# dt from the full normed x while x is prepared, in place of its hi and lo parts in a unit of its own

## Chip, cores and metric

The kernel runs on one core of a Trainium2 chip. The metric is the device time of one execution in microseconds (us). Three runs of the kernel before took 1902.75, 1903.54 and 1903.64 us; the median is 1903.54 us.

## The reference, cut to what matters

One layer of a hybrid decoder is computed for a prompt of 256 positions and for 8 sample positions that share all weights (264 columns in all). One projection of the normed input feeds every branch; 32 of its 13,856 columns are dt:

```python
def _in_proj(x, norm_mix, w_in, ...):
    h = _rmsnorm(x, norm_mix)
    q, k, v, z, xbc, dt, qm, g = jnp.split(h @ w_in, _split_points(IN_SPLITS), axis=-1)
    ...
def _ssd(xbc_raw, z, dt_raw, ...):
    dt = jax.nn.softplus(dt_raw.astype(f32) + dt_bias.astype(f32))...
    acs = jnp.cumsum(dt * a, axis=2)
    ...
```

dt sets the decays of the scan (SSD), so `_ssd` needs it before the first chunk. Keys and values of 256 memory tokens (`_mem_kv`) come from another normed input and another weight, `w_mem_kv`, and depend on nothing of x.

## The kernel before, in words

**Tiling.** Activations lie with features on the 128 partitions: 16 feature tiles (`KT`) of 128 x 264. A weight is loaded in units of 128 x 1024 (two feature tiles by 512 columns), and each unit is split into `hi` (rounded to the fast matmul type, ScalarE, L181) and `lo` (the rest, VectorE, L182). A product of two fp32 operands is three fast products: hi by hi, lo by hi, hi by lo (`group`, L303). The activations are split alike: the normed x is kept as `hh` (hi) and `hl` (lo).

**Units.** The list `units` holds the whole program's weight units in the order in which TensorE takes them: 32 units for memory keys and values (`mem_group`, products `pmem`, 128 x 512), then the projection (products `pin`, 128 x 264), then the up-projections, the output and the feed-forward. The main loop (L1746) keeps up to four units' loads (`feed`, L268, issued on SyncE) and three units' splits ahead of TensorE. PSUM has five banks for such products (`dps`) and three for side work (`sps`).

**Side work.** Everything else (norms, attention, the scan) are generators in two queues (`side`, `slow`, L1719 to L1735). After each unit the loop takes a step of them; some groups wait for a task (`XDRAIN`, L1432). A scheduler with its own model of time then orders the instructions of each engine; what is marked `keep_in_program_order` keeps its own order among such marks, yet other instructions may be set between.

**x.** `prep_x` (L465) runs beside the memory units. It sums squares, finds the reciprocal norm (`rsqrt`, VectorE), spreads it over the partitions (product `rbx`, L492, copied to `rb` by ScalarE, L494), and then for each of the 16 feature tiles transposes x on TensorE (`xT`, L505, two transposes each), copies it from PSUM (`xr`, ScalarE, L506), multiplies it with the norm (`xn`, VectorE, L508, a `t1` buffer of one tile) and splits it into `hh` and `hl` (L509). The loop demands its end at unit 30 (L1754); the first `pin` unit is unit 32.

**dt.** `dt_group` (L1446) is one unit of its own, between the group of C and the first group of x columns. It loads the 128 x 512 weight of dt's 32 columns (16 feature tiles), copies it as it is (L284, "whole") and makes 32 products in full fp32, each with 32 output rows: for each of four rounds, four feature tiles with `hh`, then the same four with `hl`. The four products of a round write four different quarters of the 128 output partitions of `pdt`, so `task_dt` (L1188) later sums the quarters (`dtT`, L1200). ScalarE copies `pdt` to `dtraw` (L1465). `task_dt` runs after the tasks of B and C.

**Quarter-width products.** A product with 32 output rows is built for a quarter of TensorE's columns (128 x 32); the quarter is the one of its output partitions. `ssq` (L676) is of the same kind.

Of the kernel before, what the change touches and what calls it, by code (L numbers as in the profile page):

```python
# [8 lines left out]
F32 = mybir.dt.float32  # L9
# [3 lines left out]
AF = mybir.ActivationFunctionType  # L13
# [5 lines left out]
P = 128  # L19
# [3 lines left out]
NT = NP + NS  # L23
KT = D // P
# [53 lines left out]
def tile_hybrid_decoder_step(  # L78
# [33 lines left out]
    def ev(name):  # L112
        return tp.tile([P, 4, NT], F32, tag="ev", name=nm(name), bufs=4)

    def const(shape, name, dt=F32, tag=None):
        return cp.tile(shape, dt, tag=tag or name, name=name)
# [29 lines left out]
    def t1(name, dt=F32):  # L146
        return tp.tile([P, NT], dt, tag="t1", name=nm(name), bufs=4)
# [5 lines left out]
    def dps(name):  # L153
        return pd.tile([P, 512], F32, tag="d", name=nm(name))
# [122 lines left out]
    def do_split(n):  # L277
        if n < state["split"]:
            return
        raw = raws.pop(n)  # L280
        hi = wp.tile([P, 1024], F32R, tag="hi", name=nm("hi"), bufs=3)
        lo = wp.tile([P, 1024], F32R, tag="lo", name=nm("lo"), bufs=3)
        if units[n].get("whole"):
            act(hi.bitcast(F32)[:, 0:512], raw[:, 0:512], AF.Copy)  # L284
        elif units[n].get("perm"):
            for k in range(2):
                v = [t[:, k * 512:(k + 1) * 512].rearrange("p (r a d) -> p a r d", r=4, a=2) for t in (hi, lo)]
                s = raw[:, k * 512:(k + 1) * 512].rearrange("p (a r d) -> p a r d", a=2, r=4)
                state["split_at"], state["rest_at"] = split(v[0], v[1], s)
        else:  # L290
            for k in range(2 if n == 0 else 1):
                c = slice(512 * k, 512 * k + 512) if n == 0 else slice(0, 1024)
                with tc.issue_after(state["memh", k if n == 0 else 1].ins):
                    state["split_at"], state["rest_at"] = split(hi[:, c], lo[:, c], raw[:, c])
        parts[n] = (hi, lo)
        state["split"] = n + 1
# [165 lines left out]
    for n, (t, h) in ((9, (1, 0)), (10, (0, 1)), (11, (1, 1))):  # L462
        behind[n] = [lambda t=t, h=h: load_x_rows(t, h)]

    def prep_x():  # L465
        xs = x_t["s"]
        jk = t2("jkx", BF16)
        ss = tiny("ssx", 6)
        act(jk[:, 0:P], xs, AF.Square, accum_out=ss[:, 4:5])
        for t in range(2):  # L470
            for h in range(2):
                act(jk, x_t[t, h], AF.Square, accum_out=ss[:, 2 * t + h:2 * t + h + 1])
            yield 0.5
        sel = tiny("sel", NS)
        V.tensor_reduce(sel, ident.rearrange("p (k b) -> p b k", b=NS), axis=AX.X, op=ALU.add)
        V.tensor_scalar(sel, sel, ss[:, 4:5], None, op0=ALU.mult)
        ps = sps("xn")
        tr(ps[:, 0:P], xs)
        mm(ps[:, P:P + NS], ones, sel)
        v = tiny("vx", 10)  # L480
        V.tensor_tensor(v[:, 0:2], ss[:, 0:4:2], ss[:, 1:4:2], op=ALU.add)
        V.tensor_copy(v[:, 2:10], ps[:, P:P + NS])
        xsT = t1("xsT")[:, 0:P]
        act(xsT, ps[:, 0:P], AF.Copy)
        V.tensor_scalar(v, v, 1.0 / D, EPS, op0=ALU.mult, op1=ALU.add)
        r = rsqrt(v, 10)
        yield 1.5
        dg = t1("dgx")[:, 0:256]
        for t in range(2):
            V.tensor_scalar(dg[:, t * P:(t + 1) * P], ident, r[:, t:t + 1], None, op0=ALU.mult)  # L490
        ps = sps("rbx")
        mm(ps[:, 0:NP], ones, dg)  # L492
        rb = t1("rb")
        act(rb[:, 0:NP], ps[:, 0:NP], AF.Copy)  # L494
        V.tensor_copy(rb[:, NP:NT], r[:, 2:10])
        yield 0.5
        for q in range(4):
            raw = ev("xr")
            V.tensor_copy(raw[:, :, NP:NT], xsT[:, 32 * q:32 * q + 32].rearrange("p (c b) -> p c b", b=NS))
            for c in range(4):  # L500
                k = 4 * q + c
                h, o = k // 8, (k % 8) * P
                ps = sps("xT")
                for t in range(2):
                    tr(ps[:, t * P:(t + 1) * P], x_t[t, h][:, o:o + P])  # L505
                act(raw[:, c, 0:NP], ps[:, 0:NP], AF.Copy)  # L506
                tm = t1("xn")
                V.scalar_tensor_tensor(tm, raw[:, c], g_mix[:, k:k + 1], rb, op0=ALU.mult, op1=ALU.mult)  # L508
                split(hh(k), hl(k), tm)  # L509
                yield 0.6  # L510
            nc.gpsimd.dma_start(xT_d[:, 4 * q:4 * q + 4], raw)


    tri = const([P, P], "tri")
# [580 lines left out]

    ssd = {}
    dt_tok = const([P, 64], "dt_tok")
    last = const([P, 11, 24], "last")
    acs_tok = const([P, 64], "acs_tok")
    wf = const([P, 96], "wf")  # L1100

# [6 lines left out]
    def conv(ct, raw, dst):  # L1108

        acc = t4("acc").rearrange("p (c n) -> p c n", c=4)  # L1110
        for c in range(4):
            ch = ct + c
            act(acc[:, c], raw[:, c], AF.Identity, scale=cw[:, 72 + ch:73 + ch], bias=c_bias[:, ch:ch + 1])
            for k in (2, 1, 0):
                o = 3 - k
                V.scalar_tensor_tensor(acc[:, c, o:NP], raw[:, c, 0:NP - o], cw[:, k * 24 + ch:k * 24 + ch + 1],
                                       acc[:, c, o:NP], op0=ALU.mult, op1=ALU.add)
            yield 1.3
        V.tensor_tensor(acc[:, :, NP:NT], acc[:, :, NP:NT], pre[:, ct:ct + 4], op=ALU.add)
        act(dst, acc, AF.Silu)  # L1120
        V.tensor_copy(last[:, :, ct:ct + 4].rearrange("p r c -> p c r"), raw[:, :, NP - 3:NT])
        if ct == 12:
            ps = sps("rawT")
            lf = last.rearrange("p r c -> p (r c)")
            for i, (o, n) in enumerate(((0, 72), (72, 96), (168, 96))):
                tr(ps[0:n, i * P:(i + 1) * P], lf[:, o:o + n])
            rows = t2("rawT")
            act(rows[0:72, 0:P], ps[0:72, 0:P], AF.Copy)
            act(rows[0:96, P:3 * P], ps[0:96, P:3 * P], AF.Copy)
            nc.scalar.dma_start(p_conv[0, 0].rearrange("r (c n) -> (r c) n", n=P), rows[0:72, 0:P])  # L1130
            for i in range(2):
                nc.scalar.dma_start(s_conv[0, 4 * i:4 * i + 4, 2].rearrange("b (c n) -> b c n", n=P),
                                    rows[0:96, (i + 1) * P:(i + 2) * P])
        yield 0.3
# [8 lines left out]
        return f  # L1143

    def task_b():
        ssd["B"] = const([P, 4, NT], "BT")
        yield from conv(16, ssd["Braw"], ssd["B"])
        bt = const([P, 2, 512], "Btok")
        for t in range(2):
            ps = sps("Btok")  # L1150
            for g in range(4):
                tr(ps[:, g * P:(g + 1) * P], ssd["B"][:, g, t * P:(t + 1) * P])
            act(bt[:, t], ps, AF.Copy)
        ssd["Btok"] = bt
        yield 0.2
# [32 lines left out]
    def task_dt():  # L1188
        ssd["dsc"] = const([P, 16, 17], "dsc", tag="nd")
        s3 = const([P, 3, 16, NS], "s3", tag="kT")  # L1190
        ssd["xsS"], ssd["zsS"], ssd["ysS"] = (s3[:, i] for i in range(3))
        raw = ssd["dtraw"]
        x = tiny("dtx", 64)

        sm = t1("dtsum")[:, 0:P]
# [233 lines left out]
            split(ssd[f"s{g}"][:, 0:4, NP:NT], ssd[f"s{g}"][:, 4:8, NP:NT], t[:, 4 * g:4 * g + 4])  # L1429
        yield 3  # L1430

    XDRAIN = ("W", "dt", "N0", "N1")  # L1432

    def x_group(g):
        h_group(C_X + 512 * g, after_xbc(f"x{g}"), before=lambda: side.drain(XDRAIN[g]))
# [1 line left out]
    def z_group(g, before=None, middle=None):  # L1437
# [4 lines left out]
            ssd[f"z{g}"] = z  # L1442
            side.ready.add(f"z{g}")
        h_group(C_Z + 512 * g, f, before=before, middle=middle)

    def dt_group():  # L1446
        def loads(raw):
            return [(raw[:, 0:512].rearrange("p (k n) -> p k n", k=KT),
                     w_in[0, :, C_DT:C_DT + 32].rearrange("(k p) n -> p k n", p=P))]

        def prod(hi, lo):

            ps = dps("pdt")[:, 0:NT]
            w = hi.bitcast(F32)
            for j in range(4):
                for x in (hh, hl):
                    for q in range(4):
                        k = 4 * j + q
                        tc.keep_in_program_order(mm(ps[32 * q:32 * q + 32], w[:, 32 * k:32 * k + 32], x(k).bitcast(F32),
                                                    start=j == 0 and x is hh, stop=j == 3 and x is hl))  # L1460
            ssd["dtps"] = ps

        def after():
            raw = t1("dtraw")
            act(raw, ssd["dtps"], AF.Copy)  # L1465
            ssd["dtraw"] = raw
            side.ready.add("dt")

        units.append(dict(loads=loads, prod=prod, after=after, whole=True))


    mg = {}

# [80 lines left out]
        gates_ssd(i)  # L1554
    h_group(C_B, after_xbc("B"))
    h_group(C_C, after_xbc("C"))
    dt_group()
    x_group(0)
    z_group(0, load_m)
    up_mem(0)  # L1560
# [163 lines left out]
    slow.add("Ms", mem_sample_values())  # L1724
    side.add("W1", swa_keys(), ["kv"])
    side.add("W", swa())
    side.add("B", task_b(), ["B"])
    side.add("C", task_c(), ["C"])
    side.add("dt", task_dt(), ["dt"])
    for g in range(4):  # L1730
        side.add(f"V{g}", ssd_conv_work(g), [f"x{g}"])
        side.add(f"X{g}", ssd_chunk_work(g))
# [66 lines left out]
```

## Time and profile before

| what | number |
|---|---|
| median of three runs | 1903.54 us |
| span of the profiled execution | 1901.3 us |
| busy share of PE (matmul), PEld (weight load) | 100%, 97% |
| busy share of DVE, ACT, POOL | 62%, 50%, 6% |
| matmul records | 15359 |
| granted TensorE clock in all 40 slices | 9 tenths or more |
| DMA, mean over the span | 211 GB/s |

The page gives no other time of the profiled execution than its span, from the first instruction to the last; the median of the runs lies 2.2 us above it. A matmul record's duration overlaps with the next record's, so the spacing of starts tells what one costs, and a "busy" engine may still be spaced wider than it could be. A product in full fp32 leaves two records, a fast one leaves one. In the timeline a row that ends in "x8" merges eight records; its first number is the first one's start. L160 is the line of the helper that records every matmul, so groups are told apart by their tiles.

### The profile page before, as it was taken

How to read it: one execution, taken by the hardware profiler on the slowest of the kernel's cores; microseconds unless marked ns; L12 is line 12 of the kernel's file. 1: busy time of each engine (PE TensorE's matmuls, PEld its weight loads, DVE VectorE, ACT ScalarE, POOL GpSimd, SP SyncE). 2: the span in 40 equal slices, each digit the busy share in tenths (PEclk: the TensorE clock that was granted, in tenths of full speed). 3: DMA queues.
4: the chain of work that ended last, by engine and by line, in shares of the span. 5: the costliest groups of instructions: out<-in, count | busy, mean ns of one | idle time of the engine just before them, and what ended most of it. 6: DMA issues, size and time to landing. Idle time of an engine off the chain costs nothing.

```text
span 1901.3 us, 37640 instructions
## 1 busy us (share of the span) xinstructions
PE 1893.6 (100%) x15359; PEld 1848.2 (97%) x15359; DVE 1176.5 (62%) x2263; ACT 959.8 (50%) x1403; POOL 114.9 (6%) x237
## 2 busy tenths in 40 slices
PE   9999999999999999999999999999999999999999
PEld 7899999989999999999999999999999999999999
DVE  5755578666787868787455665555445555445554
ACT  6654466655767676764443444444334444334443
POOL 1110001011011111110000000000000000000000
PEclk9999999999999999999999999999999999999999
DMA  8776679678777777797768556665566665566654
GB/s 303 234 235 201 203 229 298 199 226 256 215 220 250 238 243 234 234 265 223 220 226 291 191 178 178 179 185 180 178 180 183 180 179 182 182 178 178 179 191 131
DMA packets 196898, 402.08 MB, mean 211 GB/s; under 512 B 16462, under 2 KB 22052, under 8 KB 196716
## 3 DMA queue, kind: packets, MB, share of 16 engines
q1 hardware_dynamic: 171856, 324.54, 56.1%
q0 software_dynamic: 19456, 69.08, 11.0%
q10 hardware_dynamic: 5412, 6.05, 0.9%
q8 instruction: 120, 1.97, 0.4%
q14 instruction: 54, 0.44, 0.1%
HBM read 375.71 MB, written 26.19 MB: 211 GB/s over the span
## 4 chain that ended last, share of the span: by engine, by line
PE 99%; DMA 1%; ACT 0%; issue 0%; SPq 0%; ACTq 0%
PE pin L160 33%; PE pu L160 14%; PE pdn L160 14%; PE pg L160 14%; PE pus L160 5%; PE pout L160 5%; PE pmem L160 4%; PE pum L160 2%; PE pua L160 2%; DMA raw<-in_w_mem_kv_dram 1%; PE py L160 1%; PE oms L160 0%; PE ps L160 0%; PE pst L160 0%; PE scm L160 0%; PE om L160 0%
## 5 line engine op out<-in xcount | busy, mean ns | idle before, releaser
L182 DVE TENSOR_TENSOR lo<-raw,hi 128x1024 fp32r<-128x1024 f32 (+1 forms) x625 | 744.9, 1194 | 586.3 <-ACT hi L181 582.3
L181 ACT ACTIVATE hi<-raw 128x1024 fp32r<-128x1024 f32 (+1 forms) x625 | 645.4, 1036 | 849.5 <-PE pin L160 203.6
L160 PE MATMUL pin<-hl,hi 128*128 128x264 f32 x1728 | 490.5, 286 | 0.0
L160 PE MATMUL pin<-hh,hi 128*128 128x264 f32 x1728 | 489.5, 286 | 0.0
L160 PE MATMUL pin<-hh,lo 128*128 128x264 f32 x1728 | 483.0, 286 | 0.0
L160 PEld LDWEIGHTS pin<-hh,hi 128*128 128x128 f32 x1728 | 325.4, 189 | 4.6 <-issue 4.2
L160 PEld LDWEIGHTS pin<-hl,hi 128*128 128x128 f32 x1728 | 325.2, 188 | 4.2 <-issue 4.0
L160 PEld LDWEIGHTS pin<-hh,lo 128*128 128x128 f32 x1728 | 320.7, 188 | 2.0 <-issue 1.6
L160 PE MATMUL pdn<-fah,hi 128*128 128x264 f32 x704 | 199.7, 285 | 0.0
L160 PE MATMUL pdn<-fal,hi 128*128 128x264 f32 x704 | 199.4, 285 | 0.0
L160 PE MATMUL pu<-h2h,hi 128*128 128x264 f32 x704 | 199.4, 284 | 0.0
L160 PE MATMUL pu<-h2l,hi 128*128 128x264 f32 x704 | 199.3, 284 | 0.0
L160 PE MATMUL pg<-h2l,hi 128*128 128x264 f32 x704 | 199.1, 285 | 0.0
L160 PE MATMUL pg<-h2h,hi 128*128 128x264 f32 x704 | 198.4, 284 | 0.0
L160 PE MATMUL pdn<-fah,lo 128*128 128x264 f32 x704 | 197.0, 284 | 0.0
L160 PE MATMUL pu<-h2h,lo 128*128 128x264 f32 x704 | 196.6, 284 | 0.0
L160 PE MATMUL pg<-h2h,lo 128*128 128x264 f32 x704 | 196.1, 284 | 0.0
L160 PEld LDWEIGHTS pu<-h2h,hi 128*128 128x128 f32 x704 | 132.8, 189 | 0.0
L160 PEld LDWEIGHTS pdn<-fah,hi 128*128 128x128 f32 x704 | 132.7, 189 | 0.0
L160 PEld LDWEIGHTS pg<-h2h,hi 128*128 128x128 f32 x704 | 132.7, 188 | 0.0
L160 PEld LDWEIGHTS pu<-h2l,hi 128*128 128x128 f32 x704 | 132.6, 188 | 0.0
L160 PEld LDWEIGHTS pdn<-fal,hi 128*128 128x128 f32 x704 | 132.6, 188 | 0.0
(520 smaller groups left out, 2923.1 us busy)
## 6 DMA issues: line engine op xcount, KB each, us to landing
raw<-in_w_in_dram SPq DMA_DIRECT2D x216, 512.0 KB
raw<-in_w_gate_dram SPq DMA_DIRECT2D x88, 512.0 KB
raw<-in_w_up_dram SPq DMA_DIRECT2D x88, 512.0 KB
raw<-in_w_down_dram SPq DMA_DIRECT2D x88, 512.0 KB
raw<-in_w_up_ssd_dram SPq DMA_DIRECT2D x32, 512.0 KB
raw<-in_w_out_dram SPq DMA_DIRECT2D x32, 512.0 KB
raw<-in_w_mem_kv_dram SPq DMA_DIRECT2D x31, 512.0 KB
ring<-in_state_ssm_dram POOLq DMA_DIRECT2D x32, 256.0 KB, 4.9
```

The costliest lines, as they stand in the source:

```text
L160: return nc.tensor.matmul(out, lhsT=lhsT, rhs=rhs, start=start, stop=stop)
L181: h = act(hi, src, AF.Copy)
L182: return h, V.tensor_tensor(lo, src, hi.bitcast(F32), op=ALU.subtract)
```

## The change: what it does

The dt unit goes. Its weight is loaded behind unit 12 into a buffer of its own (`wdt`, one of four `t2` buffers). In `prep_x` the normed tile `xn` is no longer a buffer of one tile, but a quarter of a four-tile buffer (`full`, of the four `ev` buffers that `xr` uses too). After each four tiles, four products of the quarter-width kind follow, in full fp32, of the dt weight and the full normed tile: 16 in all, where there were 32. The sum is copied to `dt["x"]` at the end of `prep_x`; that buffer is later that of `last`. `task_dt` no longer waits for a unit; it is queued ahead of the tasks of B and C, and the second x group drains C in place of dt.

```diff
         raw = raws.pop(n)
...
-        if units[n].get("whole"):
-            act(hi.bitcast(F32)[:, 0:512], raw[:, 0:512], AF.Copy)
-        elif units[n].get("perm"):
+        if units[n].get("perm"):
...
+    dt = {}
+
+    def load_dt():
+
+        dt["w"] = t2("wdt")
+        nc.sync.dma_start(dt["w"].rearrange("p (k n) -> p k n", k=KT),
+                          w_in[0, :, C_DT:C_DT + 32].rearrange("(k p) n -> p k n", p=P))
+
+    behind[12] = [load_dt]
...
         for q in range(4):
-            raw = ev("xr")
+            raw, full = ev("xr"), ev("xn")
...
-                tm = t1("xn")
+                tm = full[:, c]
                 V.scalar_tensor_tensor(tm, raw[:, c], g_mix[:, k:k + 1], rb, op0=ALU.mult, op1=ALU.mult)
                 split(hh(k), hl(k), tm)
                 yield 0.6
             nc.gpsimd.dma_start(xT_d[:, 4 * q:4 * q + 4], raw)
+            if q == 0:
+                dt["ps"] = dps("pdt")[:, 0:NT]
+            for c in range(4):
+                k = 4 * q + c
+                tc.keep_in_program_order(mm(dt["ps"][32 * c:32 * c + 32], dt["w"][:, 32 * k:32 * k + 32], full[:, c],
+                                            start=q == 0, stop=q == 3))
+        dt["x"] = const([P, NT], "dtx", tag="last")
+        act(dt["x"], dt["ps"], AF.Copy)
...
-        raw = ssd["dtraw"]
+        raw = dt["x"]
...
-    XDRAIN = ("W", "dt", "N0", "N1")
+    XDRAIN = ("W", "C", "N0", "N1")
...
-    def dt_group():
...
-            for j in range(4):
-                for x in (hh, hl):
-                    for q in range(4):
-                        k = 4 * j + q
-                        tc.keep_in_program_order(mm(ps[32 * q:32 * q + 32], w[:, 32 * k:32 * k + 32], x(k).bitcast(F32),
-                                                    start=j == 0 and x is hh, stop=j == 3 and x is hl))
...
-    dt_group()
...
+    side.add("dt", task_dt())
     side.add("B", task_b(), ["B"])
     side.add("C", task_c(), ["C"])
-    side.add("dt", task_dt(), ["dt"])
```

**Where the dt products stand on TensorE.** Before, at the end of C's group and the start of x's first group (`hi` of unit 4957 is the dt weight):

```order
L160 MATMUL pin_4680<-hl_124,hi_4879 128x264
L160 MATMUL pin_4680<-hh_122,lo_4880 128x264
L160 MATMUL pdt_5065<-hh_121,hi_4957 32x264 x4
L160 MATMUL pdt_5065<-hl_123,hi_4957 32x264 x4
L160 MATMUL pdt_5065<-hh_121,hi_4957 32x264 x4
L160 MATMUL pdt_5065<-hl_123,hi_4957 32x264 x4
L160 MATMUL pdt_5065<-hh_122,hi_4957 32x264 x4
L160 MATMUL pdt_5065<-hl_124,hi_4957 32x264 x4
L160 MATMUL pdt_5065<-hh_122,hi_4957 32x264 x4
L160 MATMUL pdt_5065<-hl_124,hi_4957 32x264 x4
L160 MATMUL pin_5117<-hh_121,hi_4986 128x264
```

Now, in the third memory group (`pmem_848` and `pmem_849` are its two output tiles), around the products of the second four feature tiles:

```order
L160 MATMUL pmem_849<-hi_766,memh_113 128x512
L160 MATMUL pmem_849<-lo_767,memh_113 128x512
L164 MATMUL xT_754<-ident,x_412 128x128
L164 MATMUL xT_754<-ident,x_442 128x128
L160 MATMUL pmem_849<-hi_766,meml_115 128x512
L160 MATMUL pmem_848<-hi_844,memh_113 128x512
L160 MATMUL pdt_670<-xn_676,wdt_506 32x264
L160 MATMUL pmem_848<-lo_845,memh_113 128x512
L160 MATMUL pdt_670<-xn_676,wdt_506 32x264
L160 MATMUL pmem_848<-hi_844,meml_115 128x512
L160 MATMUL pdt_670<-xn_676,wdt_506 32x264
L160 MATMUL pmem_849<-hi_844,memh_113 128x512
```

The 32 products of before are one block of eight rounds of four. The 16 of now stand at 16 different places: no two follow each other, seven have `pmem` rows on both sides, six stand between transposes (`xT`, `kmT`), and three have a transpose ahead and a `pmem` row behind. The last stands in the second unit of the fourth memory group.

**Where the preparation of x begins on TensorE.** Before, in the third unit of the third memory group (`pmem_846`, `pmem_847`; `hi_762` is that unit's weight):

```order
L160 MATMUL pmem_847<-hi_722,meml_115 128x512
L160 MATMUL pmem_846<-hi_762,memh_113 128x512
L160 MATMUL pmem_847<-hi_762,memh_113 128x512
L160 MATMUL rbx_578<-dgx_575,ones 128x256
L164 MATMUL xT_603<-ident,x_328 128x128
L164 MATMUL xT_603<-ident,x_383 128x128
L164 MATMUL xT_611<-ident,x_328 128x128
L164 MATMUL xT_611<-ident,x_383 128x128
L160 MATMUL pmem_846<-lo_763,memh_113 128x512
```

Now, between the second memory group's last product (`pmem_513`, ahead of this piece) and the third's first (`pmem_848`, behind it):

```order
L160 MATMUL rbx_579<-dgx_576,ones 128x256
L164 MATMUL xT_605<-ident,x_327 128x128
L164 MATMUL xT_605<-ident,x_382 128x128
L164 MATMUL xT_612<-ident,x_327 128x128
L164 MATMUL xT_612<-ident,x_382 128x128
L164 MATMUL xT_637<-ident,x_327 128x128
L164 MATMUL xT_637<-ident,x_382 128x128
L164 MATMUL xT_644<-ident,x_327 128x128
L164 MATMUL xT_644<-ident,x_382 128x128
L164 MATMUL xT_678<-ident,x_327 128x128
L164 MATMUL xT_678<-ident,x_382 128x128
L160 MATMUL pdt_670<-xn_603,wdt_506 32x264
```

`rbx` moved up by 26 `pmem` products (over two units), and five transposed tiles and the first dt product now stand with it ahead of the third memory group's first product.

**ScalarE at that place.** Before (`hi_762`, `hi_842` and `hi_871` are splits of the third, fourth and fifth unit of the group, `rb` the spread norm):

```order
L181 ACTIVATE hi_762<-raw_718 128x1024
L181 ACTIVATE hi_842<-raw_757 128x1024
L181 ACTIVATE hi_871<-raw_838 128x1024
L494 ACTIVATE rb_580<-rbx_578 128x256
L506 ACTIVATE xr_601<-xT_603 128x256
L506 ACTIVATE xr_601<-xT_611 128x256
L181 ACTIVATE hh_121<-xn_607 128x264
```

Now (`hi_766` is the third unit's split, `hi_844` the fourth's; `ssk` sums the squares of the second memory group's keys):

```order
L181 ACTIVATE hi_766<-raw_719 128x1024
L502 ACTIVATE rb_581<-rbx_579 128x256
L402 ACTIVATE jk_783,ssk_782<-pmem_512,rs_m 128x256
L514 ACTIVATE xr_602<-xT_605 128x256
L514 ACTIVATE xr_602<-xT_612 128x256
L402 ACTIVATE jk_783,ssk_782<-pmem_512,rs_m 128x256
L514 ACTIVATE xr_602<-xT_637 128x256
L514 ACTIVATE xr_602<-xT_644 128x256
L181 ACTIVATE hh_121<-xn_603 128x264
L402 ACTIVATE jk_783,ssk_782<-pmem_513,rs_m 128x256
L514 ACTIVATE xr_675<-xT_678 128x256
```

The copies `rb` and `xr` now come right behind the third unit's split, with the sums of squares among them, and the fourth unit's split stands behind all of these and four rows more.

More of the change, by code (lines that the diff above doesn't have):

```diff
@@ L1097, in tile_hybrid_decoder_step @@
     dt_tok = const([P, 64], "dt_tok")
-    last = const([P, 11, 24], "last")
     acs_tok = const([P, 64], "acs_tok")
@@ L1120, in conv @@
         act(dst, acc, AF.Silu)
+        last = ssd["last"]
         V.tensor_copy(last[:, :, ct:ct + 4].rearrange("p r c -> p c r"), raw[:, :, NP - 3:NT])
@@ L1145, in task_b @@
     def task_b():
+        ssd["last"] = const([P, 11, 24], "last")
         ssd["B"] = const([P, 4, NT], "BT")
@@ L1444, in z_group @@
         h_group(C_Z + 512 * g, f, before=before, middle=middle)
-    def dt_group():
[L1447 to L1454, printed above, removed]
-            for j in range(4):
-                for x in (hh, hl):
-                    for q in range(4):
-                        k = 4 * j + q
-                        tc.keep_in_program_order(mm(ps[32 * q:32 * q + 32], w[:, 32 * k:32 * k + 32], x(k).bitcast(F32),
-                                                    start=j == 0 and x is hh, stop=j == 3 and x is hl))
[L1461 to L1469, printed above, removed]
     mg = {}
```

## Prediction

> **What bounds the kernel now.** I read the busy shares and the chain that ended last first, then TensorE's waits, then the busy time of the stretch in which x is prepared, then the timeline of TensorE.
>
> ```profile
> PE 1893.6 (100%) x15359; PEld 1848.2 (97%) x15359; DVE 1176.5 (62%) x2263; ACT 959.8 (50%) x1403; POOL 114.9 (6%) x237
> PE 99%; DMA 1%; ACT 0%; issue 0%; SPq 0%; ACTq 0%
> ```
>
> TensorE is in 99% of the chain. That alone does not say that it never waits for something, so its own waits follow (who waited, line, for whom: us in total, times, longest):
>
> ```profile
> PE idle L160 <- DVE warm L213: 1.5, 1, 1.5
> PE memT L164 <- DMA mem<-in_mem_prompt_dram: 1.1, 1, 1.1
> PE pmem L160 <- ACT memh L348: 0.9, 1, 0.9
> ```
>
> These 3.5 us are all, and their tiles are those of the start. The stretch from the third memory group's first product to the first projection product:
>
> ```profile
> 60.80:111.00 50.20, 50.20 (x243) 41.04 (x242) 38.42 (x91) 32.59 (x66) 6.95 (x12) 1.00 0.78 245
> ```
>
> Columns after the stretch: its length, busy time of PE, PEld, DVE, ACT, POOL, granted clock, DMA share, GB/s. TensorE is busy all through at the full clock; DVE (38.42) and ACT (32.59) have room. So the stage into which the products move has no gap to take them, and neither has the stage that they leave. Every us that TensorE spends more or less there, waiting included, is a us of the kernel. I therefore add up TensorE time.
>
> **Part 1: what is removed.** The timeline of TensorE at the dt unit (start, duration, op, shape, records):
>
> ```profile
> 417.51 0.29 PE L160 MATMUL pin<-hl,hi 128*128 128x264 f32 x1
> 417.64 0.28 PE L160 MATMUL pin<-hh,lo 128*128 128x264 f32 x1
> 417.85 0.66 PE L160 MATMUL pdt<-hh,hi 128*32 128x264 f32 x8
> 418.32 0.63 PE L160 MATMUL pdt<-hl,hi 128*32 128x264 f32 x8
> ...
> 421.00 0.63 PE L160 MATMUL pdt<-hl,hi 128*32 128x264 f32 x8
> 421.55 0.39 PE L160 MATMUL pin<-hh,hi 128*128 128x264 f32 x1
> 421.78 0.28 PE L160 MATMUL pin<-hl,hi 128*128 128x264 f32 x1
> ```
>
> and the spacing of ordinary products, from one piece of the chain (start, us, what):
>
> ```profile
> 1144.05 23.39 PE pu L160 x192
> ```
>
> An ordinary product takes 23.39 / 192 = 0.122 us. From the last `pin` start ahead of the block (417.64) to the second behind it (421.78) are 4.14 us; two ordinary spacings (0.24) would be there anyway, so the block costs **3.90 us**, and that is gone. Its inside matters as much: from 418.32 to 421.00 are six rounds of four products, 0.447 us a round. Eight rounds are 3.57 us; the other 0.33 us are paid once, for going into the block and out of it. Four products of four different quarters thus run side by side: 32 of them pay for eight.
>
> **Part 2: what is added.** Sixteen products, and the built order sets them at sixteen places, one at a time. A lone one can share its round with nobody. The trace has no lone quarter-width product of this length; the nearest row is a pair, `ssq`, between ordinary products:
>
> ```profile
> 165.16 0.29 PE L160 MATMUL pin<-hh,hi 128*128 128x264 f32 x1
> 165.38 0.63 PE L160 MATMUL ssq<-sqm,ones 128*32 128x256 f32 x4
> 165.93 0.39 PE L160 MATMUL pin<-hl,hi 128*128 128x264 f32 x1
> 166.16 0.28 PE L160 MATMUL pin<-hh,lo 128*128 128x264 f32 x1
> ```
>
> 165.16 to 166.16 is 1.00 us, less 0.24: 0.76 us for two products side by side, that is, one round of 256 columns (0.447 x 256 / 264 = 0.43) and again 0.33 for in and out. The other end is a lone fp32 product of full width and 264 columns, `ss`:
>
> ```profile
> 1127.76 0.29 PE L160 MATMUL pg<-h2h,hi 128*128 128x264 f32 x1
> 1127.88 0.61 PE L160 MATMUL ss<-sqsum,ones 128*128 128x264 f32 x2
> ...
> 1128.45 0.28 PE L160 MATMUL pg<-h2h,lo 128*128 128x264 f32 x1
> ```
>
> 1127.76 to 1128.45 is 0.69, less 0.24: 0.45 us, nothing for in and out. So a lone dt product costs 0.45 us (if the quarter costs nothing to enter) to 0.77 us (0.76 and eight columns more). I take 0.77: `ssq` has the same quarter width, `ss` has not. Sixteen are **12.3 us**; at 0.45 they are 7.2. Seven follow a `pmem` product of 0.23 us where `ssq` follows one of 0.12; should entering wait that much longer, 7 x 0.11 = 0.8 comes on top, 13.1. Below 7.2, or below nothing, speaks only a product that runs beside its neighbours; that is a rival. The Trainium skill, "TensorEngine Tiling (Array Packing)", Tiling Modes, Key Properties, speaks against such a layout: changing the tiling mode, not just the tile, drains TensorE. It gives no price. The Trainium skill, "TensorE: Matmul & The Clock Gate", Part 2, says that the last column takes about 128 cycles to leave the array; as an estimate at that page's 2.4 GHz that is 0.05 us a change, and with two changes a product the sum of this part would be 16 x (0.45 + 0.11) = 9 us. The trace's 0.33 us for in and out is three times that, and the trace decides.
>
> **Part 3: a wait at the head of the third memory group.** Before, `rbx` and the first transposes stand behind 26 `pmem` products of that group, and these cover the preparation's chain. Now `rbx`, ten transposes and the first dt product stand ahead of all of them, and TensorE takes its products in order. The rows of before that price the chain, TensorE first:
>
> ```profile
> 60.59 0.39 PE L160 MATMUL pmem<-hi,meml 128*128 128x512 f32 x1
> 60.82 0.63 PE L160 MATMUL pmem<-hi,memh 128*128 128x512 f32 x2
> ...
> 66.88 0.59 PE L160 MATMUL rbx<-dgx,ones 128*128 128x256 f32 x2
> 67.31 0.60 PE L164 MATMUL xT<-ident,x 128*128 128x128 f32 x4
> 67.67 0.48 PE L160 MATMUL pmem<-lo,memh 128*128 128x512 f32 x1
> 67.98 0.40 PE L160 MATMUL pmem<-hi,meml 128*128 128x512 f32 x1
> ```
>
> then VectorE and ScalarE:
>
> ```profile
> 61.45 0.48 DVE L490 TENSOR_SCALAR dgx<-ident,rs_y 128x128 f32<-128x128 f32 x2
> 68.94 0.89 DVE L508 SCALAR_TENSOR_TENSOR xn<-xr,vgc,rb 128x264 f32<-128x264 f32 x2
> ```
>
> ```profile
> 67.58 0.37 ACT L494 ACTIVATE rb<-rbx 128x256 f32<-128x256 f32 x1
> 67.84 0.65 ACT L506 ACTIVATE xr<-xT 128x256 f32<-128x256 f32 x2
> 84.06 0.47 ACT L404 ACTIVATE jk<-pmem,rs_m 128x256 f32<-128x256 f32 x1
> 84.42 0.20 ACT L404 ACTIVATION_READ_ACCUMULATOR jk<-pmem,rs_m 128x1 f32 x1
> 84.65 0.47 ACT L404 ACTIVATE jk<-pmem,rs_m 128x256 f32<-128x256 f32 x1
> ```
>
> The second group ends, and the third begins, at 60.82. `dgx` is there at 61.45 + 0.48 = 61.9, so `rbx` waits 1.1 us. Its result is there 0.59 later (62.5); ScalarE then makes `rb` (0.26 from its start to the next one's), one sum of squares (0.59 from 84.06 to 84.65) and the first `xr` (0.37): 63.7. VectorE's `xn` takes 0.45: 64.2. The dt product, 0.77, ends at 65.0, where the third group begins: 4.2 us late. Of these, 2.3 are work: `rbx` 0.43, ten transposes at 0.11 (four cost 0.36, and the next `pmem` spacing is 0.31, not 0.23) and the dt product, counted above. The rest, **1.9 us**, is waiting. Least is the wait for `dgx` alone, 1.1. If ScalarE's and VectorE's pieces don't overlap as in these rows (0.37, 0.67, 0.65, 0.89 in place of 0.26, 0.59, 0.37, 0.45) it is 2.8.
>
> **Part 4: edits costed at nothing.**
>
> ```profile
> 398.00:400.20 2.20, 2.20 (x20) 2.20 (x20) 1.23 (x1) 1.48 (x3) 0.00 (x0) 1.00 0.82 138
> xT_d<-xr POOLq DMA_DIRECT2D x4, 528.0 KB, 5.2
> ```
>
> The dt weight's load comes in pieces of 128 bytes; I take it for the stretch 398.0 to 400.2, where the DMA engines are 0.82 busy and yet move only 138 GB/s. It moves to SyncE's queue behind unit 12. The weights queued behind it there come about 2.2 us later; loads run four units and splits three units ahead, and a memory unit lasts 12 x 0.23 = 2.8 us, so over 8 us cover it. Uncovered it costs 2.2.
> The third `xr` buffer is now the first one again, and VectorE waits with its copy, and with the fourth unit's `lo` behind it, for the store of the first (issue to landing 5.2 us): about 65.2 + 5.2 = 70.4, and the split is done by 71.7. TensorE wants it after three units (8.4), four dt products (3.1) and eight transposes (0.9): 65.0 + 12.4 = 77.4. Cover 5.7 us; without it each us costs one.
> The other dt products wait for `xn` too, but with 18 `pmem` products (4.2 us) ahead of the second, VectorE is past them. The split that goes (ScalarE), the task that moves ahead of B's and C's, and the shared buffer of `last` change the order of side work; its products cost TensorE the same wherever they stand.
>
> **Sum.** 12.3 + 1.9 - 3.9 = +10.3 us: a span of 1911.6 in place of 1901.3. The runs' median lies 2.2 us above that span; I add the difference to it: 1903.5 + 10.3 = **1913.8 us**.
>
> **Rivals.**
> 1. *Lone products pay no entry* (0.45 each, as `ss`): 7.2 + 1.9 - 3.9 = +5.2, 1908.7. For it: transposes and dt products are all fp32, and six stand between transposes. Against it: block and pair both pay 0.33. Chance 0.14. By the Trainium skill's drain ("TensorE: Matmul & The Clock Gate", Part 2; 9 us in place of 7.2, an estimate) the case would give 1910.5.
> 2. *A lone quarter-width product runs beside its full-width neighbours* and costs nothing but its issue: 1.9 - 3.9 = -2.0, 1901.5, not slower. It decides where a product costs under (3.9 - 1.9) / 16 = 0.13 us. For it: quarters do overlap each other (0.447 for four). Against it: a `pmem` product takes all columns, and `ssq` shows no overlap with its neighbours. Chance 0.05. Without the wait too: -3.9.
> 3. *More waits*: the chain of part 3 comes back at the three later blocks of four tiles, since each dt product holds TensorE until its own `xn` is made: 3 x 1.9 more, 1919.5. For it: every product waits on VectorE. Against it: covers of 4 to 6 us above. Chance 0.08.
>
> **How the numbers follow.** The forecast has 0.73. Its own bounds are 7.2 + 1.1 - 3.9 = +4.4 and 13.1 + 2.8 - 3.9 = +12.0. The range takes in rival 1 and reaches halfway to rival 3: 1907.9 to 1917.0. A measurement of this kernel tells 0.2% (3.8 us) from no change. Rival 2 holds the other side: faster 0.02 (it, without the wait), same 0.05 (it, and a lone product well under 0.45), slower 0.93.
>
> **What would show it.** Right: 32 `pdt` records in 16 lone pairs within the memory groups, each adding about 0.77 us between its neighbours; the third group's first `pmem` 4.2 us after the second's last product; no `pdt` near 418; the projection beginning about 14 us after 111. Wrong: `pdt` pairs at 0.45 or less; `pmem` rows spaced 0.23 across a `pdt`; TensorE waits at later `pdt` rows; or weight splits that come late there.

## The result and the profile after

| | median of the runs, us | profiled execution: time, span, us |
|---|---|---|
| before | 1903.22 (1902.75 to 1903.64) | 1903.5, 1901.3 |
| changed | 1920.44 (1919.79 to 1921.31) | 1920.8, 1919.0 |

The ratio is 1.0085 (95% interval 1.0073 to 1.0096): slower, by 17.2 us between the medians and 16.2 by the ratio. The forecast was 10.3 us slower and the range ended at 1917.0, so the direction was right and the size was not.

The chain that ended last, on the page of the changed kernel:

```profile
PE 95%; DMA 2%; issue 1%; DVE 1%; ACT 1%; ACTq 0%; POOL 0%; POOLq 0%; DVEq 0%
```

TensorE had 99% of the chain and now has 95%, so something else has come into it. All waits of TensorE (who waited, line, for whom: us in total, times, longest):

```profile
PE pst L160 <- DVE xw L1309: 6.6, 1, 6.6
PE pmem L160 <- ACT memh L346: 1.8, 2, 1.3
PE idle L160 <- DVE warm L213: 1.5, 1, 1.5
PE rbx L160 <- DVE rb L503: 0.9, 1, 0.9
PE memT L164 <- DMA mem<-in_mem_prompt_dram: 0.6, 1, 0.6
PE xT L164 <- ACT xr L514: 0.3, 1, 0.3
```

`rbx` and `xT` are the forecast wait at the head of the third memory group. `pst`, on top, is one that the prediction does not have. To see where the 17.7 us between the two spans arise I follow two marks through both traces, the first projection product (`pin`) and the turn of the last rows of the convolution (`rawT`); the last two columns of times are the first and the last start. Before:

```profile
L160 PE MATMUL pin<-hh,hi x1728: 278/283/472, 110.9 to 920.0; 128*128 128x264 f32 x192
L164 PE MATMUL rawT<-ident,last x3: 273/273/273, 775.5 to 775.7; 128*96 128x128 f32 x2, 128*72 128x128 f32 x1
```

and changed:

```profile
L160 PE MATMUL pin<-hh,hi x1728: 278/284/568, 124.2 to 937.7; 128*128 128x264 f32 x192
L164 PE MATMUL rawT<-ident,last x3: 271/272/273, 784.3 to 784.6; 128*96 128x128 f32 x2, 128*72 128x128 f32 x1
```

The first `pin` is 13.3 us late, `rawT` 8.8, the last `pin` 17.7. So the memory groups give 13.3, the dt unit that is gone takes 4.5 back, and after `rawT` another **8.9 us** are lost, for which the prediction has nothing.

**The memory groups.** The head of the third group:

```profile
60.12 0.40 PE L160 MATMUL pmem<-hi,meml 128*128 128x512 f32 x1
61.45 0.67 PE L160 MATMUL rbx<-dgx,ones 128*128 128x256 f32 x2 [0.93 <-DVE rb L503]
...
63.32 0.71 PE L164 MATMUL xT<-ident,x 128*128 128x128 f32 x4 [0.29 <-ACT xr L514]
63.96 0.63 PE L160 MATMUL pdt<-xn,wdt 128*32 128x264 f32 x2
64.52 0.51 PE L160 MATMUL pmem<-hi,memh 128*128 128x512 f32 x1
```

60.12 + 0.23 to 64.52 is 4.2 us, as forecast. Further into the group, lone dt products between `pmem`:

```profile
77.66 0.50 PE L160 MATMUL pmem<-lo,memh 128*128 128x512 f32 x1
78.08 0.63 PE L160 MATMUL pdt<-xn,wdt 128*32 128x264 f32 x2
78.64 0.51 PE L160 MATMUL pmem<-hi,meml 128*128 128x512 f32 x1
```

From 77.66 to 78.64 stand one `pmem` (0.23 by itself) and one dt product: 0.98 - 0.23 = 0.75 us for the product; the forecast took 0.77.

**The late loss.** TensorE around the wait:

```profile
793.88 0.39 PE L160 MATMUL pst<-Btok,xw 128*128 128x128 f32 x2
...
795.82 0.28 PE L160 MATMUL pin<-hh,lo 128*128 128x264 f32 x1
802.74 3.35 PE L160 MATMUL pst<-Btok,xw 128*128 128x128 f32 x14 [6.64 <-DVE xw L1309]
805.75 0.57 PE L160 MATMUL pin<-hh,hi 128*128 128x264 f32 x1
```

`pst` are the eight products of the last group's chunk states. The first takes `xw0`; the second takes `xw1`, and the six behind it keep their order and wait with it. VectorE makes `xw1` at 802.0 in a buffer of the `t2` tag:

```profile
L1309 DVE TENSOR_TENSOR xw<-xdt,wf x1: 693/693/693, 802.0 to 802.0; 128x512 f32<-128x512 f32 x1
```

The view of `rawT` tells who held that buffer:

```profile
L1148 ACTq DMA_DIRECT2D out_dram<-rawT x2: 906/930/953, 786.6 to 787.5; - x2
  DVE xw L1309: 7.7, 1
```

`rows = t2("rawT")` in `conv` holds the turned rows while three DMAs of ScalarE's queue store them. `t2` has four buffers and the tiles after it are `xdt`, `xdt`, `xw0` and `xw1`; so `xw1` gets the buffer of `rawT`, and VectorE waits 7.7 us until the stores, the last issued at 787.5, have left it, 14.5 us later. In the kernel before the same wait is there, and nobody waits for it. VectorE's wait, the last two stores and `xw1`, and TensorE from the first `pst` product to the other seven:

```profile
DVE xw L1292 <- DMA out_dram<-rawT: 2.5, 1, 2.5
```

```profile
L1132 ACTq DMA_DIRECT2D out_dram<-rawT x2: 665/670/675, 776.9 to 777.6; - x2
```

```profile
L1292 DVE TENSOR_TENSOR xw<-xdt,wf x1: 693/693/693, 787.9 to 787.9; 128x512 f32<-128x512 f32 x1
```

```profile
784.38 0.39 PE L160 MATMUL pst<-Btok,xw 128*128 128x128 f32 x2
...
789.23 1.72 PE L160 MATMUL pst<-Btok,xw 128*128 128x128 f32 x14
790.71 0.37 PE L160 MATMUL pin<-hh,hi 128*128 128x264 f32 x1
```

Before, 38 `pin` products filled the 4.85 us between them. In the changed kernel 15 stand there, which are through at 796.1. Fewer products are not all of it. Counted from the issue of the last store (777.6 before, 787.5 now), TensorE comes to the seven `pst` after 11.6 us before (789.2) and after 8.6 us now (796.1), and `xw1` starts after 10.3 us before (787.9) and after 14.5 us now (802.0). So TensorE comes 3.0 us earlier and the buffer 4.2 us later; less the 0.6 us by which `xw1` was ready early before, that is the 6.6 us. The seven `pst` then took 3.01 us (802.74 to 805.75) and not 1.48 (789.23 to 790.71). The stretches of the changed kernel say why (length, TensorE's busy time, granted clock, DMA share, GB/s):

```profile
796.00:800.00 4.00, 0.10 (x1) 1.00 0.90 322
800.00:802.70 2.70, 0.00 (x0) 0.51 0.06 21
802.70:806.80 4.10, 4.06 (x19) 0.50 0.42 127
806.80:809.00 2.20, 2.20 (x19) 0.98 0.41 124
```

4 us into the gap the clock fell to half and stayed there until 806.8; TensorE worked 4.1 us at half clock, which are 2 us lost. With the 6.6 us of idling that is 8.7 of the 8.9.

### The profile page after: what moved, and what is told of

The parts are those of the page before. It is cut to its first block, busy times and chain, and to the rows that moved or that the text cites. A ratio compares the mean times of both kernels' runs of the same rounds, so it can differ in the third digit from the quotient of the medians.

```text
span 1919.0 us, 37547 instructions
## 1 busy us (share of the span) xinstructions
PE 1903.1 (99%) x15327; PEld 1849.8 (96%) x15327; DVE 1176.2 (61%) x2263; ACT 956.7 (50%) x1400; POOL 113.9 (6%) x237
## 4 chain that ended last, share of the span: by engine, by line
PE 95%; DMA 2%; issue 1%; DVE 1%; ACT 1%; ACTq 0%; POOL 0%; POOLq 0%; DVEq 0%
PE pin L160 32%; PE pu L160 13%; PE pdn L160 13%; PE pg L160 13%; PE pus L160 5%; PE pout L160 5%; PE pmem L160 3%; PE pum L160 2%; PE pua L160 2%; DMA out_dram<-rawT 1%; PE py L160 1%; DMA raw<-in_w_mem_kv_dram 1%; PE pdt L160 0%; PE pst L160 0%; PE oms L160 0%
```

## The experiments

The theory (A): the mechanisms of the prediction hold, and the rest is one wait for the buffer of `rawT`, uncovered because fewer products stand in front of it, with the half clock behind it. The main rival (B): the new order of the side work costs the time, and the wait is only where it shows. Each kernel was timed beside the kernel before on the same chip, whose median there was 1903.65 to 1904.23 us. A difference to the changed kernel goes by the ratios: its 1.0085 times 1904.2 is 1920.4 us.

### rawT in tiles of its own

```diff
-            rows = t2("rawT")
-            act(rows[0:72, 0:P], ps[0:72, 0:P], AF.Copy)
-            act(rows[0:96, P:3 * P], ps[0:96, P:3 * P], AF.Copy)
+            rows72 = const([P, P], "rawT1", tag="bcs")
+            rows = const([P, 11, 24], "rawT2", tag="last").rearrange("p r c -> p (r c)")
+            act(rows72[0:72], ps[0:72, 0:P], AF.Copy)
+            act(rows[0:96, 0:2 * P], ps[0:96, P:3 * P], AF.Copy)
```

(`bcs` is one tile for `kn_bc`, `dtb_bc` and `na_bc`, which are dead by then, as is `last` once turned.) In the changed kernel:

> The changed kernel with one edit: the turned rows of the convolution state (rawT) stand in two tiles that are dead by then, not in one of the four t2 buffers. Theory A (the late loss is a buffer wait): the 8.9 us that the changed kernel loses near 796 us are xw1 waiting for the rawT stores to leave its buffer (TensorE idle 6.6 us) and the half clock that follows (about 2 us); both go: 1911.5 us (1910 to 1913), and no wait of VectorE on a rawT store is left. Rival B (the new order of the side work costs them, and the wait is only where they show): another wait takes their place, 1918 to 1921.

Measured: 1912.57 us (1912.15 to 1912.76), ratio 1.0043 (1.0031 to 1.0056). The longest waits of TensorE that are left are 1.5 and 1.3 us at the start and 0.9 of `rbx`; the other three are 0.6 us and less, and no `pst` is among them. `rawT` is turned at 784.9 and the last `pin` starts at 929.4, both 9.4 us later than before: nothing is lost in between, and the span is 1910.7. Theory A holds and B falls: one buffer is the whole late loss. The built order differs only in that `xw1`'s multiply and the seven `pst` come forward.

The same edit in the kernel before, as a control:

> The kernel before with the same edit alone, as a control. Theory A: there the same wait (2.5 us of VectorE) stands beside 38 products of TensorE and costs nothing: no change, 1902.2 to 1904.2. Rival B says nothing else of it. If the kernel before also pays for that wait, 1900.5 to 1901.5.

Measured: 1903.37 us, ratio 0.9993 (0.9985 to 1.0002). No change, although VectorE no longer waits there: before, the wait was covered whole.

### The gap filled

```diff
+                if g == 3 and j == c == 0:
+                    for _ in range(27):
+                        tc.keep_in_program_order(mm(pc[:, 3 * P:4 * P], ident, ones))
```

> The changed kernel with one edit: 27 more products of 128 x 128, whose results nobody reads, stand on TensorE between the last pin before the late wait and the seven state products (pst) behind it, some 6 us of work in a gap of 6.6 us. The wait for the rawT store stays. Theory A (the half clock from 800 to 807 us comes from TensorE standing idle): the clock stays at 1.0, the seven pst take 1.6 us and not 3.35, and about 2 us go: 1918.4 us (1917.6 to 1919.2). Rival F (the clock falls there for another reason): 1920 to 1921, or more by what the products overrun.

Measured: 1918.73 us (1917.74 to 1919.59), ratio 1.0077 (1.0064 to 1.0089). TensorE and the clock in the same stretches as above:

```profile
796.61 6.19 PE L160 MATMUL cb<-ones,ident 128*128 128x128 f32 x54
802.68 1.83 PE L160 MATMUL pst<-Btok,xw 128*128 128x128 f32 x14
804.26 0.37 PE L160 MATMUL pin<-hh,hi 128*128 128x264 f32 x1
```

```profile
800.00:802.70 2.70, 2.70 (x27) 1.00 0.17 60
802.70:806.80 4.10, 4.10 (x35) 1.00 0.46 134
```

`pst` starts where it did (802.68), takes 1.58 us, and the clock stays at 1.00. So the idling caused the half clock. By the medians that is 1.7 us; the intervals of the two ratios overlap, and the rows carry the verdict.

### What uncovered the wait

The dt task moved ahead of those of B and C, and a unit is gone. First the kernel before with the task moved:

```diff
+    side.add("dt", task_dt(), ["dt"])
     side.add("B", task_b(), ["B"])
     side.add("C", task_c(), ["C"])
-    side.add("dt", task_dt(), ["dt"])
```

(and `XDRAIN = ("W", "C", "N0", "N1")`)

> The kernel before with one edit: the dt task stands ahead of the tasks of B and C in the side work, as in the changed kernel, and the second x group drains C; the dt unit and its products stay. Theory A (the late buffer wait is uncovered because fewer projection products stand between the store and the state products, and that number changes with the missing unit, not with the order of the tasks): TensorE's order around the rawT store is that of before, and so is the time, 1902.5 to 1904.5. Rival B (putting dt ahead moves B, C and the conv work so that the wait is uncovered): 1908 to 1913.

Measured: 1904.29 us (1903.97 to 1906.85), ratio 1.0004 (0.9996 to 1.0013): no change, and 38 products stay between the `pst`. The moved task does not uncover the wait. Then the changed kernel with one more step of side work, as a step went with the unit:

```diff
-            side.step(SIDE_US)
-            slow.step(SLOW_US)
+            for _ in range(2 if i == 87 else 1):
+                side.step(SIDE_US)
+                slow.step(SLOW_US)
```

> The changed kernel with one edit: the side work, which is let go one step behind each weight unit, gets a second step behind the last unit of C, in place of the one that went with the dt unit. rawT stays in a t2 buffer. TensorE's order around the rawT store is then that of before: 96 projection products between the turn of rawT and the seven state products that wait (12, 5, 41 and 38), where the changed kernel has 78 (20, 4, 39 and 15). Theory A' (the order alone uncovers the wait): nothing is lost there, 1911.5 us (1910.5 to 1913), like rawT in dead tiles. Rival H (the store itself lands later than before, 14.4 us after its issue and not 10.3, for its company on the DMA engines): 18 products or 2.1 us of the 6.6 are covered and some 4.5 stay, with a part of the half clock: 1915.5 to 1918.

Measured: 1918.04 us (1917.74 to 1919.47), ratio 1.0075 (1.0062 to 1.0089). The time alone lies at the upper end of rival H's range; the trace says otherwise. TensorE's wait at the state products:

```profile
PE pst L160 <- DVE xw L1309: 0.6, 1, 0.6
```

The expectation puts the second step behind the last unit of C. Unit 87 is the last of the second gate group (`gates_ssd`); with 32 memory units and eight units in each of the eleven projection groups up to C, the last of C is unit 119. The step thus comes 32 units early: from the 1468th to the 2572nd `pin` product the side work on TensorE stands in an order that neither kernel has, and from the 2667th on, to the end, in the order of before.

There `pst` waits 0.6 us and not 6.6: with 38 products in between again the wait is covered nearly whole. The store lands earlier, too: `xw1` starts 11.6 us after the last store's issue (790.1 to 801.7) where it was 14.5. That goes with the order in every profiled execution that has the wait: 10.3, 10.6 and 11.6 us where 38 products stand between (before, before with the task moved, this run), 13.1 to 14.5 in the five where 15 stand (the changed kernel, the gap filled, and the three edits of the next two sections). Rival H, by which the store would still land late, falls. So one step of side work less takes the cover away.

The span is still 5.3 us above that of `rawT` in its own tiles (1916.0 against 1910.7). TensorE's waits name 3.6 of it: 0.6 here, 1.9 of `oms` (attention of the samples over memory) for a load, in the stretch whose order neither kernel has, and 0.9 and 0.2 of `pua` (an up-projection) for splits. That the step brings the last three is not shown: `oms` also waits 1.3 and 1.4 us in the profiled executions of the head edit and of full width, and `oms` and `pua` wait 1.4 and 1.2 in that of the kernel before with the task moved, all without such a step. The other 1.7 us stand in no wait that the profile names; they stay open. Theory A' was right on the wait and wrong on the time.

### The products: four in a run, and full width

The first product of a round waits for the round's last `xn`, so nothing comes between the four:

```diff
+                if c == 0:
+                    tc.add_manual_dep(d.ins, made.ins.name, mybir.DependencyInfo(
+                        mybir.DependencyClass.Sync, mybir.DependencyReason.DATA), reason="four")
```

(`made` is the `xn` of c = 3.)

> The changed kernel with one edit: the first of the four dt products of a round waits for the last of the four normed blocks, so the 16 products stand in four runs of four and not alone. Theory A (a run pays about 0.33 us for going into quarter-width products and out again, and a round of four 0.45): 4 x 0.78 = 3.1 us in place of 16 x 0.8 = 12.9, less about 1.4 us for a longer wait at the head of the third memory group: 1912 us (1910.5 to 1913.5). Rival C (each product costs about 0.8 wherever it stands): 1920 to 1922.

Measured: 1913.01 us (1911.91 to 1913.46), ratio 1.0045 (1.0031 to 1.0059). A run of four between `pmem`:

```profile
76.02 0.40 PE L160 MATMUL pmem<-hi,memh 128*128 128x512 f32 x1
76.35 0.66 PE L160 MATMUL pdt<-xn,wdt 128*32 128x264 f32 x8
76.93 0.50 PE L160 MATMUL pmem<-lo,memh 128*128 128x512 f32 x1
77.27 0.39 PE L160 MATMUL pmem<-hi,meml 128*128 128x512 f32 x1
```

76.02 to 77.27 is 1.25, less two `pmem` (0.46): 0.79 us for four products, where one alone took 0.75. The price is for the run, and the first `pin` comes 8.0 us earlier than in the changed kernel (116.2 in place of 124.2). Rival C falls.

The same products at full width (the built order leaves most of them lone and sets some in threes):

```diff
-                tc.keep_in_program_order(mm(dt["ps"][32 * c:32 * c + 32], dt["w"][:, 32 * k:32 * k + 32], full[:, c],
-                                            start=q == 0, stop=q == 3))
+                j = 32 * min(k, 12)
+                tc.keep_in_program_order(mm(dt["ps"], dt["w"][:, j:j + P], full[:, c], start=k == 0, stop=k == 15))
```

> The changed kernel with its 16 dt products made full width: each takes 128 neighbouring columns of the weight tile in place of its own 32 and writes all 128 partitions, one accumulation over all of them, so the values of dt are not computed. Theory A (what a lone product pays beside its own passes is the change into quarter width and back): a lone product costs what its two passes cost, about 0.46 us, in place of 0.82: 16 x 0.36 = 5.8 us less than the changed kernel, 1914.6 us (1913 to 1916). Rival C (any lone plain fp32 product between others costs about 0.8): 1919.5 to 1921.

Measured: 1916.31 us (1915.27 to 1918.2), ratio 1.0065 (1.0052 to 1.0078), just above the range.

```profile
91.53 0.61 PE L160 MATMUL pdt<-xn,wdt 128*128 128x264 f32 x2
91.78 0.58 PE L160 MATMUL pmem<-hi,meml 128*128 128x512 f32 x1
92.20 0.39 PE L160 MATMUL pmem<-hi,memh 128*128 128x512 f32 x1
92.43 0.61 PE L160 MATMUL pdt<-xn,wdt 128*128 128x264 f32 x2
```

91.53 to 92.43 is 0.90, less 0.46: 0.44 us, as `ss` in the prediction's rows. So quarter width costs 0.31 us a product more (0.75 - 0.44). The expectation took 0.82 for the lone product, read with a transpose behind it; 16 x 0.31 is 5.0 us. By the medians 4.1 came; in the profiled execution the first `pin` comes 4.5 us earlier (119.7 in place of 124.2), and behind it this execution differs in other things, a late wait of 5.4 us in place of 6.6, 3.4 us of half clock in place of 6.8, and 1.4 us in which `oms` waits for a load.

### The head of the third group

```diff
+        while "rbx" not in side.ready:
+            yield None
         ps = sps("rbx")
...
+        if i == 14:
+            side.ready.add("rbx")
```

> The changed kernel with one edit: the second half of the preparation of x is let go later, so that rbx and the first transposes stand behind 26 products of the third memory group as in the kernel before. Theory A: the products and transposes cost what they cost, and only the 1.9 us of waiting at the head of the group go: 1918.5 us (1917.5 to 1919.3). Rival D (the wait is paid later in that stage in another form, by the splits of the normed x): 1919.8 to 1921.

Measured: 1918.27 us (1917.45 to 1918.84), ratio 1.0073 (1.0061 to 1.0086), 2.2 us under the changed kernel. Neither `rbx` nor `xT` waits any more, and the first `pin` comes at 122.1 in place of 124.2. The 1.9 us of waiting were a term of their own. Rival D falls by the trace; the intervals alone would not decide.

### All three, and longer runs

> The changed kernel with three edits together: rawT in dead tiles, the dt products in four runs of four, and rbx behind 26 products of the third memory group. Theory A: the three gains add, since they are three places: 8.0 + 7.5 + 2.1 us off 1920.4, 1902.8 us (1901 to 1904), level with the kernel before. Rival E (they share cover, and part of one is lost with another): 1904.5 to 1907.

Measured: 1902.99 us (1902.4 to 1904.34), ratio 0.9992 (0.9983 to 1.0001): the three gains add, and undo the loss. One product of the full x in place of two of its parts is then worth nothing that can be measured. Two runs of eight in place of four of four:

> The kernel with the three edits together, and the dt products in two runs of eight in place of four runs of four (the normed blocks of two rounds are kept until then). Theory A (a run pays 0.33 us for the way in and out, a product 0.11): 2 x 1.22 = 2.4 us in place of 4 x 0.79 = 3.2, so 0.7 us less than the three edits alone, 1902.3 us, about 0.1% under the kernel before of the same chip (ratio 0.998 to 1.0). Rival G (waits for the later normed blocks take the 0.7 us back): level with the three edits or above, ratio 0.9992 or more.

Measured: 1904.23 us (1903.82 to 1905.25), ratio 1.0003 (0.9994 to 1.0012). Rival G. The runs themselves cost what was expected:

```profile
107.24 0.40 PE L160 MATMUL pmem<-hi,meml 128*128 128x512 f32 x1
107.56 1.10 PE L160 MATMUL pdt<-xn,wdt 128*32 128x264 f32 x16
108.59 0.50 PE L160 MATMUL pmem<-hi,memh 128*128 128x512 f32 x1
108.93 0.41 PE L160 MATMUL pmem<-lo,memh 128*128 128x512 f32 x1
```

(1.69 - 0.46 = 1.23 us for eight), but the first of them stands behind the transposes and waits for the eighth `xn`:

```profile
89.34 1.10 PE L160 MATMUL pdt<-xn,wdt 128*32 128x264 f32 x16 [1.51 <-DVE xn L519]
```

No version here beats the kernel before by what can be measured.

## Why the prediction was right or wrong

1. *What bounds the kernel.* Right: every us of TensorE counted, and each edit above moved the time by TensorE's time. But that nothing behind the start makes TensorE wait was read from the kernel before, and outside the stage of part 3 it was carried over to the changed one.
2. *Part 1, the block that goes, -3.9.* Between the first `pin` and `rawT` the changed kernel gains 4.5 on the kernel before (13.3 to 8.8). Right: the first `pin` behind the block's place starts at 421.55 before and at 431.11 now, 9.56 us late, where the first `pin` of all is 13.34 late (110.86 and 124.20). So 3.8 us go at the block itself. The other 0.7 comes in small steps up to `rawT`, with the side work in another order and no wait that the profile names; why was not tried.
3. *Part 2, sixteen lone products, +12.3.* Right. 0.75 us each is 12.0, by the `ssq` row and not by `ss`; the runs of four and the full width show that the price is for going into quarter width and back. Rivals 1 and 2 fall with it.
4. *Part 3, the wait at the head, +1.9.* Right: the third group began 4.2 us late, the profile names 1.2 us of that as waits (0.93 and 0.29), and the edit that lets `rbx` go later took 2.2 us back. Rival 3, the chain again at the later blocks, did not come: TensorE has no other wait on `xn` or `xr`.
5. *Part 4, "change the order of side work; its products cost TensorE the same wherever they stand".* **This step failed.** The products cost the same; what they cover does not. The unit that went took a step of side work with it, 15 products stood where 38 had covered the wait for the buffer of `rawT`, the store left that buffer 4.2 us later, and 6.6 us of idling and 2 us of half clock came up. The prediction named cover for the load, the `xr` buffers and the other products, but for side work it named none, and did not look for waits of VectorE and ScalarE in the trace of before that were covered only just. The 2.5 us of VectorE on `rawT` were such a wait, and the built order of the changed kernel shows the 15 products. That the store would land later no built order shows, so the size of the loss could not be read ahead of the run; that the cover shrank could.
6. *The sum.* With the late loss, 10.3 + 8.9 = 19.2 against 17.7 between the spans. The 1.5 left: the third group began its lateness 0.5 earlier than before (60.12 in place of 60.59 for the product ahead of it), 0.6 more came back between the first `pin` and `rawT`, the memory groups took 0.4 less than forecast. The range was worked out from the terms that were listed; nothing in it stood for a term that was not. Its upper end is given as halfway to rival 3, which is 1916.7 and not 1917.0; nothing hangs on it.

## What to carry to other kernels

A wait that costs nothing is covered by something: list the waits of the engines off the path, with what stands in front of who needs them, and count that again in the order of the changed kernel. A step removed from a loop that also paces other work moves that other work, however little the step did itself. Put products of a smaller tile in runs: four together cost hardly more than one.

## What the runs showed of the hardware

- In the changed kernel, which is otherwise busy, the granted clock fell to half 3.9 us after TensorE's last product (796.1 to 800.0) and came back 4.1 us after it had work again (802.7 to 806.9); a 6.6 us wait thus cost 8.7. The fall does not come after a fixed time: in the three other profiled executions with this wait it came 2.5 us (four in a run), 2.1 us (head) and 5.1 us (full width) after the last product, and the full clock 4.2, 3.4 and 3.1 us after work was back. The half clock lasted 6.8, 6.8 and 3.4 us, in the changed kernel 6.8. The Trainium skill, "TensorE: Matmul & The Clock Gate", Part 1, gives half clock after an idle window of about 3.4 us, and the same span of work to come back, on a window that runs freely; the lengths of the half clock agree with one and two such windows, but the falls after 2.1 and 2.5 us came before 3.4 us of idling, and the measurement decides. In the gap that was filled the clock stayed at 1.00: products whose results nobody reads hold it.
- Going from full-width into quarter-width products and back cost 0.31 to 0.35 us, whether one, four or eight stood between (0.75, 0.79 and 1.23 us, less 0.44 us for each round of up to four). The Trainium skill, "TensorEngine Tiling (Array Packing)", Tiling Modes, says of this that the change of mode drains TensorE.
- Three stores of 36 and 48 KB in pieces of 512 bytes held their buffer for 10.3 us from the last issue before (777.6 to 787.9), 11.6 in the run with the extra step and 14.5 in the changed kernel. The mean DMA share in those stretches was 1.01, 0.93 and 0.85. What made the difference beyond the order was not tried.
